# A two-layer trunk: eight row sums moved from the first gated network to attention's output product, two more inner tiles by block products, and the value weights at another offset

## The chip, the cores and the metric

The kernel runs on one core of a Trainium2 chip, in one launch. The metric is the device time of one execution in microseconds (us). The core has five engines that work side by side, each through its own list of instructions in order: PE multiplies matrices, DVE and ACT work on elements, POOL is a third and slower element engine, and SP only issues transfers. The program's order on each engine is fixed when it is built, so an instruction that waits holds up everything behind it on its engine.

## The reference, cut to what matters

```python
def adaln_params(c, w, b):
    mod = jax.nn.silu(c) @ w + b
    shift, scale, gate = jnp.split(mod, 3, axis=-1)
    ...
def modulate(x, g, shift, scale):
    return rmsnorm(x, g) * (1.0 + scale) + shift

def conv_ffn(h, w_up, conv_w, conv_b, w_down):
    up = h @ w_up
    a, b = jnp.split(up, 2, axis=-1)
    ...                                   # causal depthwise conv of width 3 on a
    return (jax.nn.silu(a_conv) * b) @ w_down

def reference(x, c, ...):
    h = x
    for i in range(DEPTH):                # 2 layers: S5 mixer, then forgetting attention
        shift, scale, gate = adaln_params(c, ada_w[i, 0], ada_b[i, 0])
        hn = modulate(h, norm_g[i, 0], shift, scale)
        m = s5_mixer(hn, ...) if i % N_MIXERS == 0 else fox_mixer(hn, ...)
        h = h + gate * m
        shift, scale, gate = adaln_params(c, ada_w[i, 1], ada_b[i, 1])
        hn = modulate(h, norm_g[i, 1], shift, scale)
        h = h + gate * conv_ffn(hn, ...)
    return rmsnorm(h, final_g)
```

The sequence has 512 positions, the model 1024 channels, the gated network 2816 inner channels, all in float32. The attention projects queries, keys, values and forget gates, makes a causal softmax over 16 heads and ends with an output product by a 1024 x 1024 matrix.

## The kernel before, in words

**Stages.** One after the other: the S5 mixer, the first gated network (below: the first network), attention (values, then eight pairs of heads with the projection of queries and keys between them, then the output product), the second gated network, and the last norm. The residual stream `h` stays on the chip as 8 channel tiles of 128 x 512.

**Products.** A float32 product is made of three products in a shorter format, `hi*hi + hi*lo + lo*hi`. So each weight that arrives (`raw`, 128 x 1024, or `rawd`, a single buffer of its own, for the down projection inside the first network) is split: ACT writes the rounded part `w_hi` (line 277), DVE the rest `w_lo` (line 278), and PE needs both. Line 294 holds the plain matmuls, 512 columns each or 256 in halves.

**Inner tiles.** The inner channels are 22 tiles, f = 0 to 21, in groups of 4, 4, 5, 4 and 5. A plain tile takes 48 matmuls of 512 columns. The others are made by `quarters()`: seven block products in place of eight, with 84 matmuls of 256 columns (line 550), four sums of weights on DVE (`sums`, line 518), a third split weight, and copies of block results by ACT (`nm_h`, line 557) which DVE combines (line 518 again). The tuple `plain` says which tiles are plain. The down projection of one group (line 294 too, and line 362 for the residual on DVE) is woven into the next group's inner tiles.

**Row sums.** The modulation parameters of later sub-layers are made in the background: `ada_units` (lines 217 to 260) has for each 128 channels a load of 512 KB (line 233) and one long DVE instruction that multiplies 128 x 1024 numbers and sums each row (line 247), and after eight of them one small addition (line 254). A call of `tick(n)` lets n steps of this list be recorded. With `late=True` a load is issued from POOL's queue after the sum that frees its buffer, with as many loads ahead as there are rooms; with `late=False` from SP's, one fewer ahead. The first network's list holds 32 row sums, two per inner tile from f = 4 on. Attention has three lists with 7, 7 and 2 sums, the last of them in the output product, at the evacuations of its tiles 4 and 5.

**Order.** A scheduling layer turns the recorded work into each engine's order by its own costs and due times. Therefore a change in the recorded steps also moves instructions around it.

**Places of split weights.** `part_of` gives each split weight a room of 9 x 128 elements, and the weight begins a few elements in: at `ASIDE` = 22 (88 bytes) where 256 columns are multiplied, at `VALUES` in attention's values (line 1366), where the split weights are the moving operand, with 256 or 272 columns.

**Output product.** `fox()` at its end multiplies by `fox_w_out`: the first four output tiles together (`head=4`, one step per k, between which the last pair of heads is finished), then tiles 4 and 5, and tiles 6 and 7 in halves (`tail=2`). The squares of the new `h` feed the next norm (lines 391 to 430), whose result `a_hi`, `a_lo` opens the second network.

Of the kernel before, what the change touches and what calls it, by code (L numbers as in the profile page):

```python
# [17 lines left out]
P = 128  # L18
D = 1024
KT = D // P  # L20
S = 512
# [28 lines left out]
units = lambda *thirds: [(i, t, j) for i, t in thirds for j in range(D // P)]  # L50
# [10 lines left out]
    pool.tile([P, n // 4], F32, name="fill", bufs=1)  # L61


ROOM, ASIDE, VALUES = 9 * P, 22, P - 22


def part_of(pool, shape, name, tag, bufs, aside=0):
# [1226 lines left out]
class Kernel(S5):  # L1294
# [93 lines left out]
    def fox(self, i, x, nxt):  # L1388
        with self.tc.tile_pool(name="fox", bufs=1, reuse_waits="tile") as pool:
            self.bgpool = pool  # L1390
            self.fox_heads(pool, x)
            after, y = nxt
            residual = self.add_residual(i)

            def add(m, ps, cols):
                residual(m, ps, cols)
                if m in (4, 5):
                    self.tick(1)

            self.product(  # L1400
                self.io["fox_w_out"], range(KT), KT, lambda k: (self.o[k][:, 0], self.o[k][:, 1]),
                add, head=4, tail=2, after=after, halves=(slice(0, S),), step=self.unit,
            )
        return y

# [133 lines left out]
def build(tc, io, out, stop=None):  # L1539
    with ExitStack() as ctx:  # L1540
        k = Kernel(tc, io, ctx)
        x = k.s5(0, k.norm_mod(1))
        if stop == "s5":
            return k.dump(out)
        k.done()
        k.bg = [k.ada_units(units(*((2, t) for t in range(3)), (3, 2)))]
        x = k.ffn(1, 0, x, k.norm_mod(2), ticks=1, plain=(0, 1, 2, 3, 6, 11, 17))
        k.done()
        k.bg = [
            k.ada_units(units((3, 1))[:7], rooms=("s3", "phi", "plo"), late=False),  # L1550
            k.ada_units(units((3, 1))[7:] + units((3, 0))[:6], rooms=(1, 2), late=False),
            k.ada_units(units((3, 0))[6:], rooms=("s3", "nf"), late=False),
        ]
        if stop == "ffn0":
            return k.dump(out)
        x = k.fox(2, x, k.norm_mod(3))
        k.done()
        k.mods.close()
        if stop == "fox":
            return k.dump(out)  # L1560
        k.ffn(3, 1, x, k.norm_out(out), plain=(0, 1, 2, 3))
        k.finish_norm()
# [83 lines left out]
```

## Time and profile before

| what | us |
|---|---|
| median of 3 runs | 1212.53 (1211.41 to 1212.78) |
| profiled execution, its own time | 1215.46 |
| span of that execution | 1213.7 |
| PE busy in it | 1183.8 (98%) |
| DVE busy | 1004.6 (83%) |
| ACT busy | 610.0 (50%) |
| POOL busy | 85.8 (7%) |
| row sums of the first network, first to last | 321.3 to 564.7 |
| attention's values (PE) | 617.8 to 668.0 |
| attention's output product, to the first matmul of the second network | 817.4 to 863.0 |

The page divides the span in 40 slices of 30 us. PE reads 9 (90% or more) in all but the first and the last slice, and DVE 7 to 9 in most. A row of the timeline has the start and the duration of an instruction in us, the engine, the line, what it writes and reads, and in brackets the engine's idle time before it with what ended it. A row of the windows has the length of the stretch and, for each engine, the busy time in it and the number of instructions, then the granted PE clock as a share, the share of busy transfer engines and GB/s.

### The profile page before, as it was taken

To read this page: it belongs to the slowest core of one execution; us is meant where nothing else is said; L and a number is where in the kernel's file an instruction comes from. 1 tells how busy PE (TensorE), PEld (TensorE's weight loads), DVE (VectorE), ACT (ScalarE), POOL (GpSimd) and SP (SyncE) were. 2 spreads that over 40 slices of the span, in tenths; PEclk is the share of its full clock that TensorE was granted. 3 is DMA by queue.
4 is the path that set the end of the run, shared out by engine and by line. 5 is a ranking of instruction groups with operands and counts; after the bars stand their busy time and mean duration, and the time that the engine had idled before them with its cause. 6 is when DMAs were issued, how large, how long until landed. Compare 5 with 4: busy or idle time off the path is not lost.

```text
span 1213.7 us, 20336 instructions
## 1 busy us (share of the span) xinstructions
PE 1183.8 (98%) x7793; PEld 1015.9 (84%) x7793; DVE 1004.6 (83%) x1872; ACT 610.0 (50%) x1156; POOL 85.8 (7%) x145
## 2 busy tenths in 40 slices
PE   6999999999999999999999999999999999999997
PEld 2566678898988899789899888878989999999987
DVE  7799987689899988899788578876899887888865
ACT  3554565335545453445443565764466554555543
POOL 0000000100000000000000343520000000000000
PEclk9899999999999999999999999999999999999999
DMA  9588787531364544544435453432213332333331
GB/s 356 188 266 258 245 271 253 202 99 53 122 204 156 179 163 155 161 159 130 131 125 194 162 173 134 150 109 88 89 55 111 117 121 84 104 103 109 109 100 70
DMA packets 74513, 183.81 MB, mean 151 GB/s; under 512 B 23232, under 2 KB 25632, under 8 KB 73392
## 3 DMA queue, kind: packets, MB, share of 16 engines
q1 hardware_dynamic: 68367, 161.02, 40.5%
q0 software_dynamic: 5760, 20.97, 5.4%
q8 instruction: 61, 1.00, 0.3%
q10 hardware_dynamic: 288, 0.52, 0.1%
q14 instruction: 37, 0.30, 0.1%
HBM read 175.57 MB, written 6.92 MB: 150 GB/s over the span
## 4 chain that ended last, share of the span: by engine, by line
PE 62%; issue 26%; DVE 4%; DMA 4%; POOL 2%; ACT 1%; SPq 0%; POOLq 0%; DVEq 0%; ACTq 0%
PE mmp L294 25%; PE mmp L550 11%; PE aux L550 4%; PE mmp L1174 3%; PE mmp L1366 3%; PE mmp L1203 2%; PE aux L1505 1%; PE aux L1525 1%; POOL ada_raw L233 1%; PE aux L1065 1%; PE mmp L205 1%; DMA ada_raw<-in_ada_t 1%; PE aux L978 1%; PE aux L1057 1%; DVE w_lo L278 1%
## 5 line engine op out<-in xcount | busy, mean ns | idle before, releaser
L278 DVE TENSOR_TENSOR w_lo<-raw,w_hi 128x1024 fp32r<-128x1024 f32 (+4 forms) x173 | 183.2, 1064 | 37.6 <-ACT w_hi L277 37.1
L277 ACT ACTIVATE w_hi<-raw 128x1024 fp32r<-128x1024 f32 (+4 forms) x173 | 154.8, 905 | 102.0 <-PE mmp L294 44.5
L294 PE MATMUL mmp<-ghi,w_hi 128*128 128x512 f32 (+1 forms) x392 | 145.1, 370 | 0.0
L294 PE MATMUL mmp<-ghi,w_lo 128*128 128x512 f32 (+1 forms) x392 | 144.3, 368 | 0.7 <-DVE w_lo L278 0.5
L294 PE MATMUL mmp<-glo,w_hi 128*128 128x512 f32 (+1 forms) x392 | 144.6, 369 | 0.0
L294 PE MATMUL mmp<-a_hi,w_hi 128*128 128x512 f32 (+1 forms) x376 | 138.4, 371 | 1.5 <-ACT a_hi L433 1.5
L294 PE MATMUL mmp<-a_hi,w_lo 128*128 128x512 f32 (+1 forms) x376 | 136.1, 362 | 0.3 <-DVE w_lo L278 0.3
L294 PE MATMUL mmp<-a_lo,w_hi 128*128 128x512 f32 (+1 forms) x376 | 135.7, 362 | 0.0
L550 PE MATMUL mmp<-w_hi 128*128 128x256 f32 x396 | 109.9, 278 | 3.0 <-ACT nm_h L557 2.5
L550 PE MATMUL mmp<-w_hi,w_lo 128*128 128x256 f32 x396 | 109.7, 278 | 0.7 <-DVE w_lo L278 0.7
L550 PE MATMUL mmp<-w_lo,w_hi 128*128 128x256 f32 x396 | 109.5, 277 | 0.0
L557 ACT ACTIVATE nm_h<-mmp 128x256 f32<-128x256 f32 x99 | 37.2, 381 | 108.3 <-PE mmp L550 108.3
L278 DVE TENSOR_TENSOR w_lo<-sums,w_hi 128x1024 fp32r<-128x1024 f32 x74 | 90.1, 1220 | 0.0
L277 ACT ACTIVATE w_hi<-sums 128x1024 fp32r<-128x1024 f32 x74 | 77.0, 1054 | 25.3 <-DVE sums L518 23.4
L294 PEld LDWEIGHTS mmp<-ghi,w_lo 128*128 128x128 f32 x392 | 74.2, 189 | 13.9 <-DVE w_lo L278 1.4
L294 PEld LDWEIGHTS mmp<-ghi,w_hi 128*128 128x128 f32 x392 | 74.2, 189 | 11.9 <-ACT w_hi L277 0.6
L294 PEld LDWEIGHTS mmp<-glo,w_hi 128*128 128x128 f32 x392 | 74.2, 189 | 11.0
L294 PEld LDWEIGHTS mmp<-a_hi,w_hi 128*128 128x128 f32 x376 | 70.2, 188 | 13.2 <-ACT a_hi L433 1.9
L294 PEld LDWEIGHTS mmp<-a_hi,w_lo 128*128 128x128 f32 x376 | 70.6, 188 | 12.5 <-DVE w_lo L278 1.3
L294 PEld LDWEIGHTS mmp<-a_lo,w_hi 128*128 128x128 f32 x376 | 70.7, 188 | 9.7
L362 DVE SCALAR_TENSOR_TENSOR h<-mmp,par,h 128x512 f32<-128x512 f32 (+1 forms) x100 | 68.1, 683 | 11.8 <-PE mmp L294 11.6
L550 PEld LDWEIGHTS mmp<-w_hi 128*128 128x128 f32 x396 | 74.5, 188 | 3.6 <-ACT nm_h L557 2.9
(319 smaller groups left out, 3082.2 us busy)
## 6 DMA issues: line engine op xcount, KB each, us to landing
raw<-in_w_up SPq DMA_DIRECT2D x88, 512.0 KB, 3.4
raw<-in_ada_w SPq DMA_DIRECT2D x40, 512.0 KB, 6.4
ada_raw<-in_ada_t POOLq DMA_DIRECT2D x40, 512.0 KB, 3.9
nf<-nfd SPq DMA_DIRECT2D x8, 1152.0 KB, 7.8
raw<-in_fox_qk SPq DMA_DIRECT2D x16, 512.0 KB, 3.6
raw<-in_w_down SPq DMA_DIRECT2D x24, 320.0 KB, 3.2
rawd<-in_w_down SPq DMA_DIRECT2D x24, 256.0 KB, 3.3
raw<-in_w_down SPq DMA_DIRECT2D x16, 384.0 KB, 3.4
```

The source lines that it names most:

```text
L205: self.last_mm = nc.tensor.matmul(ps[32 * qq:32 * qq + 32, :], self.sc32[:, k, :], w[:, q * S:(q + 1) * S], start=(step is steps[0]), stop ...
L233: (nc.gpsimd if late else nc.sync).dma_start(ws[n], src)
L277: nc.scalar.activation(hi, src, AF.Copy)
L278: return nc.vector.tensor_tensor(lo, src, hi.bitcast(F32), ALU.subtract)
L294: self.last_mm = self.nc.tensor.matmul(o, wt, xt[:, cols], start=(k == 0 and n == 0), stop=(k == nk - 1 and n == 2),)
L362: add = self.nc.vector.scalar_tensor_tensor(self.h[:, m, cols], ps, self.par[i][:, 16 + m:17 + m], self.h[:, m, cols], op0=ALU.mult, op1=A ...
L550: self.last_mm = nc.tensor.matmul(o, wt[:, k], xt[:, k], start=(first and k == 0 and n == 0), stop=(k == H - 1 and n == 2), skip_group_che ...
L557: a = nc.scalar.activation(t, o, AF.Copy)
L978: nc.tensor.matmul(ps[:, :, cols], x[:, q, r].rearrange("p c j -> p (c j)"), both[:, :, planes, q, :], start=(r == 0), stop=(r == 1), skip ...
L1174: nc.tensor.matmul(ps, w[m][:, k, :], x[:, k], start=(k == 0), stop=(k == KT - 1))
L1203: nc.tensor.matmul(gps[m], wt, xt[:, k], start=(k == 0 and part == 0 and xt is yhi), stop=(k == KT - 1 and part == 1))
L1366: self.last_mm = nc.tensor.matmul(ps[q, b][:, :n], xt[:, k, tb], wt, start=(k == 0 and i == 0), stop=(k == KT - 1 and i == 2),)
```

## The change

Three edits, which meet in the plan of the two stages.

1. Tiles f = 11 and f = 17 leave `plain`, so they too are made by block products.
2. The eight sums of unit (3, 2), the gate of the second network, leave the first network's list, which then has 24, and join attention's last list, which then has 10 in place of 2. This list is now `late=True`: its loads come from POOL's queue. Its steps are recorded at the seventh and eighth step of the first four output tiles (2 and 3 ticks) and at the evacuations of tiles 0 to 5.
3. `VALUES` goes from 106 elements (424 bytes) to 16 (64 bytes).

```diff
-ROOM, ASIDE, VALUES = 9 * P, 22, P - 22
+ROOM, ASIDE, VALUES = 9 * P, 22, 16
...
+            calls = []
+
+            def step(n=1):
+                self.unit(n)
+                calls.append(n)
+                if len(calls) in (KT - 1, KT):
+                    self.tick(2 + len(calls) - KT + 1)
+
             def add(m, ps, cols):
                 residual(m, ps, cols)
-                if m in (4, 5):
+                if m < 6:
                     self.tick(1)
...
-                add, head=4, tail=2, after=after, halves=(slice(0, S),), step=self.unit,
+                add, head=4, tail=2, after=after, halves=(slice(0, S),), step=step,
...
-        k.bg = [k.ada_units(units(*((2, t) for t in range(3)), (3, 2)))]
-        x = k.ffn(1, 0, x, k.norm_mod(2), ticks=1, plain=(0, 1, 2, 3, 6, 11, 17))
+        k.bg = [k.ada_units(units(*((2, t) for t in range(3))))]
+        x = k.ffn(1, 0, x, k.norm_mod(2), ticks=1, plain=(0, 1, 2, 3, 6))
...
-            k.ada_units(units((3, 0))[6:], rooms=("s3", "nf"), late=False),
+            k.ada_units(units((3, 0))[6:] + units((3, 2)), rooms=("s3", "nf")),
```

**How it moves instructions.** In the rows below stand the line, the operation, what is written from what, and the shape. `ISA` on line 247 is a row sum. Line numbers behind the edit are 8 higher in the changed kernel.

DVE in the output product, before, from the end of the last pair of heads (`ot` is its result, `v` the split of it; buffer numbers are kept, and the three `w_lo` are the weights of output tiles 5, 6 and 7):

```order
L1532 TENSOR_TENSOR ot_8709<-ot_8709,aux_8710 64x512
L1532 TENSOR_TENSOR ot_8709<-ot_8709,aux_8721 64x512
L278 TENSOR_TENSOR v_6346<-ot_8709,v_6346 128x512
...
L356 TENSOR_TENSOR ssq_8759<-ssq_8759,nm_t_8762 128x512
L278 TENSOR_TENSOR w_lo_8812<-raw_8813,w_hi_8811 128x1024
L356 TENSOR_TENSOR ssq_8759<-ssq_8759,nm_t_8766 128x512
L278 TENSOR_TENSOR w_lo_8849<-raw_8850,w_hi_8848 128x1024
L356 TENSOR_TENSOR ssq_8759<-ssq_8759,nm_t_8770 128x512
L278 TENSOR_TENSOR w_lo_8855<-raw_8856,w_hi_8854 128x1024
...
L247 ISA s3_8695,ada_s_7410<-s3_8695,c_row_1933 128x1024
```

and in the changed kernel (the instruction that stores each sum, and a few others, left out):

```order
L247 ISA nf_8803,ada_s_7516<-nf_8803,c_row_1933 128x1024
...
L247 ISA s3_8801,ada_s_7516<-s3_8801,c_row_1933 128x1024
...
L1540 TENSOR_TENSOR ot_8817<-ot_8817,aux_8818 64x512
...
L247 ISA nf_8858,ada_s_8873<-nf_8858,c_row_1933 128x1024
...
L278 TENSOR_TENSOR v_6452<-ot_8817,v_6452 128x512
L247 ISA s3_8855,ada_s_8873<-s3_8855,c_row_1933 128x1024
...
L247 ISA nf_8878,ada_s_8873<-nf_8878,c_row_1933 128x1024
...
L247 ISA s3_8875,ada_s_8873<-s3_8875,c_row_1933 128x1024
...
L278 TENSOR_TENSOR w_lo_8946<-raw_8947,w_hi_8945 128x1024
L247 ISA nf_8887,ada_s_8873<-nf_8887,c_row_1933 128x1024
...
L247 ISA s3_8881,ada_s_8873<-s3_8881,c_row_1933 128x1024
...
L278 TENSOR_TENSOR w_lo_8981<-raw_8982,w_hi_8980 128x1024
```

All ten row sums now stand between the last `plo` and the third `w_lo`: six ahead of the first `w_lo`, two between the first and the second, two between the second and the third. Of the two sums that stood here before, both came behind the third `w_lo`.

POOL at the end of the last pair of heads, before (line 1496 scales the softmax's rows) and in the changed kernel:

```order
L1453 TENSOR_TENSOR nf<-nf,rest 128x2x2x128
L1453 TENSOR_TENSOR nf<-nf,rest 128x2x256
L1496 TENSOR_SCALAR s_8581<-s_8581,sm 128x128 x2
L1496 TENSOR_SCALAR s_8591<-s_8591,sm 128x256 x2
L1496 TENSOR_SCALAR s_8601<-s_8601,sm 128x384 x2
L1496 TENSOR_SCALAR s_8611<-s_8611,sm 128x512 x2
```

```order
L1504 TENSOR_SCALAR s_8687<-s_8687,sm 128x128 x2
L1504 TENSOR_SCALAR s_8697<-s_8697,sm 128x256 x2
L233 DMA nf<-in_ada_t 128x1024
L1504 TENSOR_SCALAR s_8707<-s_8707,sm 128x384 x2
L1504 TENSOR_SCALAR s_8717<-s_8717,sm 128x512 x2
L233 DMA s_8801<-in_ada_t 128x1024
L233 DMA nf<-in_ada_t 128x1024
L233 DMA s_8855<-in_ada_t 128x1024
```

Ten loads of 512 KB are now issued from POOL, alternating between the rooms `nf` and `s`; before, two were issued from SP here.

ACT in the last group of inner tiles of the first network, around the block tile f = 18, before:

```order
L277 ACTIVATE w_hi<-rawd 128x512
L277 ACTIVATE ghi<-conv 128x512
L277 ACTIVATE w_hi<-rawd 128x512
L557 ACTIVATE nm_h<-mmp 128x256 x3
L277 ACTIVATE w_hi<-raw 128x1024
```

and in the changed kernel:

```order
L605 ACTIVATE conv<-conv 128x512
L277 ACTIVATE ghi<-conv 128x512
L557 ACTIVATE nm_h<-mmp 128x256 x3
L277 ACTIVATE w_hi<-rawd 128x512
L277 ACTIVATE w_hi<-raw 128x1024
```

The copies of block results (`nm_h`) stood behind the second split of the pair of `rawd` weights; now they stand ahead of it.

## The prediction, on record before the changed kernel ran

> **What bounds the kernel now.** I read the page's busy shares first, then windows stage by stage, then the rows around each stop of PE.
>
> ```profile
> span 1213.7 us, 20336 instructions
> PE 1183.8 (98%) x7793; PEld 1015.9 (84%) x7793; DVE 1004.6 (83%) x1872; ACT 610.0 (50%) x1156; POOL 85.8 (7%) x145
> ```
>
> PE sets the end: it is idle for 1213.7 - 1183.8 = 29.9 us in all. So a saving has to shorten PE's work or remove one of its few stops, and DVE, second at 83%, can make a new stop wherever it is filled. That is read by stage. The windows of the first network's groups 2 to 5 and of attention's values (PE, PEld, DVE, ACT, POOL busy, then clock, transfer share, GB/s):
>
> ```profile
> 305.29:366.60 61.31, 61.31 (x396) 55.63 (x395) 54.98 (x85) 30.42 (x49) 3.17 (x6) 1.00 0.52 165
> 366.60:439.63 73.03, 72.24 (x481) 65.44 (x480) 68.53 (x110) 35.57 (x58) 5.28 (x10) 1.00 0.53 174
> 439.63:507.87 68.24, 66.52 (x458) 60.74 (x457) 56.18 (x89) 30.69 (x51) 4.24 (x8) 1.00 0.44 145
> 507.87:579.21 71.34, 68.00 (x457) 62.33 (x456) 64.67 (x100) 32.50 (x54) 3.69 (x7) 0.98 0.47 151
> 617.76:668.00 50.24, 50.24 (x407) 49.50 (x407) 43.00 (x122) 21.57 (x40) 1.14 (x3) 1.00 0.50 168
> ```
>
> The group at 305 has no stop of PE with DVE at 90%. The one at 366 (f = 8 to 12, with the plain tile 11) has DVE at 68.53 of 73.03, 94%. The one at 507 (f = 17 to 21) has stops of 3.34 us and is the only one with a lower clock.
>
> **Term 1: what a tile gains.** Windows with the matmuls of one tile alone (PE, PEld, clock, transfers), a block tile, a plain tile, and the block tile f = 18:
>
> ```profile
> 320.18:329.73 9.55, 9.55 (x84) 9.50 (x83) 1.00 0.51 173
> 335.19:346.07 10.88, 10.88 (x49) 9.01 (x48) 1.00 0.73 239
> 522.09:536.04 13.95, 11.44 (x84) 11.21 (x83) 0.88 0.45 150
> ```
>
> A block tile takes 9.55 us and a plain one 10.88 (one of its 49 is a neighbour's): 1.33 us less PE work per tile, 2.7 for both, if DVE can follow. What it costs DVE, by the start-to-start times where DVE is full:
>
> ```profile
> 426.12 1.22 DVE L247 CUSTOM_DVE_ANT_0 ada_raw<-ada_raw,c_row 128x1024 f32<-128x1024 f32 x1
> 427.26 0.69 DVE L518 TENSOR_TENSOR sums<-sums,raw 128x512 f32<-128x512 f32 x1
> 427.86 0.69 DVE L518 TENSOR_TENSOR sums<-raw 128x512 f32<-128x512 f32 x1
> 432.80 0.42 DVE L518 TENSOR_TENSOR nm_t<-mmp,nm_h 128x256 f32<-128x256 f32 x1
> 433.13 1.22 DVE L278 TENSOR_TENSOR w_lo<-sums,w_hi 128x1024 fp32r<-128x1024 f32 x1
> ```
>
> From 426.12 to 427.26 is 1.14 for 1024 columns, to 427.86 is 0.60 for 512, 432.80 to 433.13 is 0.33 for 256. A block tile adds four sums (2.40) and four combinations (1.32), and splits 3.5 weights (1.14 + 1.14 + 1.14 + 0.60 = 4.02) where a plain tile splits two (2.28): 5.46 us in all. For the group at 366 this makes 68.53 + 5.5 = 74.0 us of DVE against 72.24 - 1.33 = 70.9 of PE. DVE is then the longer; its work may slip into the next group, where it has 68.24 - 56.18 = 12 us free. So f = 11 gives between -1.4 (all slips) and +2.5 (DVE's 74.0 plus the 1.5 it now leaves idle, against 73.03). I take -0.3, near the hidden end, because the group at 305 hides 90% wholly and this one must hide more.
>
> **Term 2: the last group.** Its largest stop:
>
> ```profile
> 523.59 0.69 DVE L278 TENSOR_TENSOR w_lo<-rawd,w_hi 128x512 fp32r<-128x512 f32 x1
> 524.30 5.31 SPq L183 DMA_DIRECT2D rawd<-in_w_down  x2
> 527.90 0.63 ACT L277 ACTIVATE w_hi<-rawd 128x512 fp32r<-128x512 f32 x1 [3.57 <-DMA rawd<-in_w_down]
> 528.44 0.64 ACT L557 ACTIVATE nm_h<-mmp 128x256 f32<-128x256 f32 x2
> 528.86 0.38 PE L550 MATMUL mmp<-w_hi 128*128 128x256 f32 x1 [2.50 <-ACT nm_h L557]
> 508.77 0.50 PE L294 MATMUL mmp<-a_hi,w_lo 128*128 128x512 f32 x1 [0.29 <-DVE w_lo L278]
> ```
>
> Read from the bottom of the chain: PE waits 2.50 for the copy `nm_h`. That copy stands on ACT behind a split that waits 3.57 for `rawd`, whose load could start at 524.30 only, once a late DVE had split the buffer's last content (523.59). The tile takes 13.95 instead of 9.55: 2.5 of stop and 1.9 at a granted clock of 0.88, 4.4 together. In the changed kernel DVE has eight row sums less here (8 x (1.14 + 0.08 of read-out) = 9.8) and 5.5 more for f = 17, so 64.67 - 4.3 = 60.4 against PE's 65.4 - 1.3 = 64.1 (65.4: 4 x 9.55 + 10.88 + 72 more matmuls of 10.88 / 48); and the copies stand ahead of that split. So I expect DVE in time: the group loses 71.34 - 65.4 = 5.9 now, of which the 4.4 and some 0.2 of the small stops go (4.6), and the tile's 1.33: -5.9. Its ends: -2.0, the tile's 1.33 and the small stops, if a like stop forms at another tile, as the group at 439 has 1.7 with DVE at 82%; -7.3 if every stop goes.
>
> **Term 3: the output product.** The rows of its DVE, and the one load that matters:
>
> ```profile
> 828.17 0.33 SPq L233 DMA_DIRECT2D s<-in_ada_t  x1
> 828.38 1.29 DVE L278 TENSOR_TENSOR plo<-aux,phi 128x512 fp32r<-128x512 f32 x2 [2.59 <-ACT phi L277]
> 832.77 0.68 DVE L1532 TENSOR_TENSOR ot<-ot,aux 64x512 f32<-64x512 f32 x1 [3.10 <-ACT ot L1531]
> 835.46 0.69 DVE L278 TENSOR_TENSOR v<-ot,v 128x512 fp32r<-128x512 f32 x1 [0.70 <-ACT v L277]
> 836.97 2.83 DVE L362 SCALAR_TENSOR_TENSOR h<-mmp,par,h 128x512 f32<-128x512 f32 x4 [0.82 <-PE mmp L294]
> 843.91 1.22 DVE L278 TENSOR_TENSOR w_lo<-raw,w_hi 128x1024 fp32r<-128x1024 f32 x1
> 860.27 0.87 DVE L430 SCALAR_TENSOR_TENSOR nm_h<-h,ga,aux 128x256 f32<-128x256 f32 x2 [0.47 <-PE aux L410]
> 862.96 0.36 PE L294 MATMUL mmp<-a_hi,w_hi 128*128 128x256 f32 x1
> ```
>
> DVE is free here: 2.59 + 3.10 + 0.70 + 0.82 us before 837, which is where eight more sums could go. But their loads come through two rooms, each refilled after its sum, and the row sums of the first network show that cycle:
>
> ```profile
> 522.99 0.08 DVE L247 DVE_READ_ACCUMULATOR2_ANT ada_s<- 128x1 f32 x1
> 523.37 0.53 POOL L233 DMA_DIRECT2D ada_raw<-in_ada_t  x1 [8.43 <-DVE ada_s L247]
> 527.22 1.22 DVE L247 CUSTOM_DVE_ANT_0 ada_raw<-ada_raw,c_row 128x1024 f32<-128x1024 f32 x1 [0.47 <-DMA ada_raw<-in_ada_t]
> ada_raw<-in_ada_t POOLq DMA_DIRECT2D x40, 512.0 KB, 3.9
> raw<-in_w_up SPq DMA_DIRECT2D x88, 512.0 KB, 3.4
> DMA to landing us min/median/max: 3.4/3.9/8.1
> ```
>
> A sum that has stored its result at 523.07 finds the next content at 527.22: 4.15, plus 1.22 + 0.08 for itself is 5.4 us per room. The `s` room is free at 828.17, as before; its first content is there at 828.17 + 3.9 = 832.1 and its five sums start at 832.1, 837.5, 842.9, 848.3 and 853.7. `w_lo` of tile 5 stands behind the third, with 0.60 and 0.66 between: done at 846.6. That of tile 6 is done at 852.0, and that of tile 7, behind the fifth, at 857.0; before it was 845.1 (843.91 + 1.22). A tile takes PE 24 x 10.88 / 48 = 5.4 us, the same as the cycle, so it stays just ahead of its weights; I put its three waits at 0.8, 0.5 and 0.5. Behind them on DVE come the splits for the second network (five, 5.7 us), the residuals and the eleven small steps of the norm, which before were done at 860.27. I put the first matmul of the second network at 869.4 instead of 862.96: +6.4, of which 1.8 is at the tiles and the rest waits for the norm. The ends: +2.1, if the loads are never late (10.0 us of sums less the 7.2 of holes just named, less 0.7 of idle later), and +9, if that wait also lowers the clock by what the 2.5 stop above did (1.9) and the splits all fall in front of the norm.
>
> The issues move from SP to POOL, behind scalings whose last row in the trace is this:
>
> ```profile
> 820.35 1.36 POOL L1496 TENSOR_SCALAR s<-s,sm 128x512 f32<-128x512 f32 x2
> ```
>
> They are done by 821.7; SP's queue gets shorter by two. Both cost nothing, because the rooms come free later than that; without this cover the first two sums would be 0.5 late, one issue.
>
> **Term 4: 64 bytes.** The rows of the values, and of another product, whose two operands begin at multiples of 64 bytes by the program's layout:
>
> ```profile
> 641.71 0.28 PE L1366 MATMUL mmp<-w_hi,a_hi 128*128 128x256 f32 x1
> 642.91 0.28 PE L1366 MATMUL mmp<-w_lo,a_hi 128*128 128x256 f32 x1
> 695.45 0.28 PE L1525 MATMUL aux<-phi,v 128*128 128x256 f32 x1
> 695.57 0.28 PE L1525 MATMUL aux<-plo,v 128*128 128x256 f32 x1
> ```
>
> The first two are ten steps apart: 120 ns each at 424 bytes. Line 1525 takes 120 ns too, while line 550 takes 9.55 / 84 = 114 with its stationary operand at 88 bytes. The nearest row, also with 256 columns as the moving operand, says that nothing changes: 0. The ends: +0.3, and -2.6, if 288 steps fall by 6.6 ns and the 96 wider ones by 7. [...]
>
> **The sum.** -0.3 - 5.9 + 6.4 + 0 = +0.2 on the profiled execution's 1215.46. That one lies 2.9 above the median 1212.53, so the forecast is 1212.7: no change that can be measured. For this kernel 0.2%, 2.4 us, is about what a measurement can tell from none.
>
> **Rivals.**
>
> *A, the loads are in time: faster.* The output product costs +2.1 only; then 1212.5 - 6.2 + 2.1 = 1208.4. For it: DVE's holes of 7.2 us, and a landing of 3.4 at the least, which makes the cycle 4.9. Against: with it the fifth sum of the `s` room still starts at 853.7 - 4 x 0.5 = 851.7, later than tile 7's weights were done. Chance 0.26.
>
> *B, the 64 bytes count.* -2.6 more: 1210.1. For it: line 550 shows that 256 columns can go in 114 ns. Against: line 1525. Chance 0.08.
>
> *C, the loads are late: slower.* The place is the `s` room's chain of four refills, and each is followed by `w_lo` on the same engine. A landing of 4.9 instead of 3.9 puts tile 7's weights and the norm 4 us later: 1216.7; the largest landing, 8.1, would add 4.2 for one refill. From 4.5 on it decides (4 x 0.6 = 2.4). For it: that maximum, and DVE full in front of each issue. Against: transfers are less busy here than in the groups above. Chance 0.21. [...]
>
> *D, the last group keeps its stop.* The single `rawd` buffer stays, and DVE's order may make it late at another tile: term 2 is then -2.0, and 1212.5 - 0.3 - 2.0 + 6.4 = 1216.6. For it: the group at 439 stops with DVE at 82%. Chance 0.07.
>
> **Numbers.** The forecast itself has 0.38, with a range of its own of 1209 to 1216. Of that 0.26 lies within 0.2%, 0.07 below and 0.05 above. A gives 0.25 faster, B 0.07, C and D together 0.27 slower, and each of these three 0.01 within. Together: faster 0.39, same 0.29, slower 0.32. The range of 1206 to 1219 holds A and C and most of the bounds: all four terms at one end together (1212.5 - 1.4 - 7.3 + 2.1 - 2.6 = 1203) are unlikely, and so is a load of 8 us in each cycle.
>
> **What will show it.** Term 1: line 550 at f = 11 in 9.6 us, DVE over 95% in that group, its length 73 or less. Term 2: no PE stop over 1 us after 508, and a length of 65 to 66. Term 3: row sums of one room 5.4 apart with a DMA as releaser, tile 7's `w_lo` near 857 less what was saved before, and a PE stop of 4 to 5 us ahead of the second network. Term 4: steps of line 1366 at 120. I am wrong if the output product adds less than 3 us or more than 9, or if the last group saves less than 3.

## The result, and the profile after

The changed kernel takes 1219.33 us (median of 18 runs, 1212.55 to 1227.79), the kernel before, on the same chips, 1212.18 (18 runs, 1209.63 to 1214.94). The ratio is 1.0057, with a 95% interval of 1.0042 to 1.0072: some 7 us slower. The forecast was 1212.7 with a range up to 1219. The profiled execution of the change was the fastest of its 18, so its page alone would have said the opposite:

```profile
span 1210.7 us, 20528 instructions
PE 1176.8 (97%) x7865; PEld 1014.9 (84%) x7865; DVE 1014.4 (84%) x1892; ACT 616.5 (51%) x1168; POOL 88.3 (7%) x147
```

PE is busy for 7 us less than before (1183.8), and the span is only 3 us shorter. Not all of the 7 is less work: the two tiles are worth 2.7 by term 1, and a matmul at a low clock counts as busy for longer (in the change, matmuls of 256 columns are 0.214 us apart and 0.41 long from 858.14 to 861.13, where the clock is at 0.50, and 0.115 apart and 0.28 long from 861.49 on, where it is at 1.00); the first profile of before has more low clock (last section). Because executions of one program differ, the stages below are means over three profiles each: of before, the one shown, one more, and that of a version with the same instruction order (the value weights at 64 bytes); of the change, the one shown and two more. The bounds are matmuls: the first block product, the first of line 1366, the last logits of the last pair of heads, the first matmul of the second network, the last matmul of all.

| stage | before, three profiles | change, three profiles | difference of the means |
|---|---|---|---|
| S5 and the first tiles | 299.9, 295.2, 295.6 | 294.3, 299.0, 299.2 | +0.6 |
| first network | 317.8, 317.4, 319.6 | 308.1, 308.4, 310.7 | -9.2 |
| values and heads | 199.3, 199.3, 199.1 | 198.5, 200.0, 198.9 | -0.1 |
| output product | 45.9, 45.8, 45.8 | 55.5, 56.1, 56.5 | +10.2 |
| second network and end | 342.8, 342.8, 343.8 | 346.5, 347.2, 346.2 | +3.5 |

The sum is +5.0, just below what the runs say (+5.1 to +8.7). The gain in the first network is larger than I forecast; the output product takes all of it, and the second network, whose own plan the change does not touch, loses 3.5 more.

The windows of the change for the groups from f = 4, 8, 13 and 17, and for the end of the first network, columns as in the prediction:

```profile
299.64:361.54 61.90, 61.53 (x396) 55.65 (x395) 55.23 (x85) 30.64 (x49) 3.18 (x6) 1.00 0.52 165
361.54:433.29 71.75, 68.87 (x508) 64.18 (x506) 69.03 (x114) 34.83 (x60) 5.30 (x10) 1.00 0.47 156
433.29:501.55 68.26, 68.26 (x467) 62.53 (x466) 65.31 (x102) 35.38 (x57) 3.72 (x7) 1.00 0.52 168
501.55:565.68 64.13, 64.13 (x493) 61.23 (x492) 56.60 (x88) 33.99 (x58) 0.00 (x0) 1.00 0.34 103
565.68:602.36 36.68, 35.25 (x222) 31.37 (x221) 26.30 (x53) 15.65 (x27) 0.00 (x0) 1.00 0.43 135
```

The last group went from 71.34 to 64.13 us without a single stop: DVE has 56.6 us of work in it instead of 64.67. In the group of f = 8 to 12 DVE is at 96%, and PE has two stops of about 1 us that were not there before, both for a late `w_lo`:

```profile
409.74 0.39 PE L550 MATMUL mmp<-a_hi,w_lo 128*128 128x256 f32 x1 [1.05 <-DVE w_lo L278]
419.05 0.50 PE L294 MATMUL mmp<-ghi,w_lo 128*128 128x512 f32 x1 [1.06 <-DVE w_lo L278]
```

Even so this group is 1.3 us shorter (71.75 against 73.03), because part of DVE's work slipped into the next one, where it is busy for 65.31 us instead of 56.18 and stops nobody.

Now the output product of the change. First DVE: the five sums of the `s` room, with all its waits for them grouped, then the split for output tile 7:

```profile
816.49 1.22 DVE L247 CUSTOM_DVE_ANT_0 s<-s,c_row 128x1024 f32<-128x1024 f32 x1 [1.69 <-DMA s<-in_ada_t]
821.84 1.23 DVE L247 CUSTOM_DVE_ANT_0 s<-s,c_row 128x1024 f32<-128x1024 f32 x1 [0.84 <-DMA s<-in_ada_t]
827.84 1.23 DVE L247 CUSTOM_DVE_ANT_0 s<-s,c_row 128x1024 f32<-128x1024 f32 x1 [0.93 <-DMA s<-in_ada_t]
833.24 1.23 DVE L247 CUSTOM_DVE_ANT_0 s<-s,c_row 128x1024 f32<-128x1024 f32 x1 [0.62 <-DMA s<-in_ada_t]
839.60 1.23 DVE L247 CUSTOM_DVE_ANT_0 s<-s,c_row 128x1024 f32<-128x1024 f32 x1 [0.42 <-DMA s<-in_ada_t]
841.49 1.22 DVE L278 TENSOR_TENSOR w_lo<-raw,w_hi 128x1024 fp32r<-128x1024 f32 x1
L247 DVE CUSTOM_DVE_ANT_0 s<-s,c_row 128x1024 f32<-128x1024 f32 x5 | 6.1, 1225 | 4.5 <-DMA s<-in_ada_t 4.5
```

The sums are 5.35, 6.0, 5.4 and 6.4 us apart, each behind a load. Behind them the norm of the second network has to pass DVE, step by step between splits of weights that it does not need yet (the first and the last step of the norm's root, and two splits between them):

```profile
848.51 0.15 DVE L391 TENSOR_SCALAR rs_v<-aux 128x2 f32<-128x2 f32 x1
849.82 1.22 DVE L278 TENSOR_TENSOR w_lo<-raw,w_hi 128x1024 fp32r<-128x1024 f32 x1 [0.16 <-ACT w_hi L277]
852.10 1.23 DVE L278 TENSOR_TENSOR w_lo<-raw,w_hi 128x1024 fp32r<-128x1024 f32 x1 [0.53 <-ACT w_hi L277]
853.83 0.16 DVE L401 TENSOR_TENSOR rs_y<-rs_y,rs_t 128x2 f32<-128x2 f32 x1
```

PE waits for that last step, and then runs slowly. The row of the waiting matmul before; then, in the change, its row and the window behind it, with the granted clock in the third column from the right:

```profile
859.55 0.68 PE L410 MATMUL aux<-rest,rs_y 128*128 128x128 f32 x4 [0.26 <-DVE rs_y L401]
```

```profile
854.13 0.81 PE L410 MATMUL aux<-rest,rs_y 128*128 128x128 f32 x4 [3.95 <-DVE rs_y L401]
854.13:864.13 10.00, 9.74 (x56) 9.45 (x57) 7.12 (x27) 4.07 (x8) 0.00 (x0) 0.66 0.16 57
```

The same window in the two other profiles of the change:

```profile
860.92:870.92 10.00, 9.73 (x46) 9.45 (x47) 6.85 (x26) 4.06 (x8) 0.00 (x0) 0.53 0.18 55
```

```profile
862.82:872.82 10.00, 9.74 (x51) 9.45 (x52) 6.85 (x26) 4.07 (x8) 0.00 (x0) 0.59 0.18 56
```

and the ten microseconds from the start of the second network before:

```profile
862.96:873.00 10.04, 9.58 (x82) 9.24 (x81) 8.48 (x27) 3.92 (x9) 0.00 (x0) 1.00 0.24 77
```

Before, matmuls of the last half tile stood behind the norm's matmul and filled the time until the norm was through (859.99 to 862.6); in the change they end at 850.2, ahead of it, and nothing is left to run. PE looks busy in both kernels, but in the change at 0.53 to 0.66 of the clock: 10 x (1 - 0.66) = 3.4, 4.7 and 4.1 us of work are lost behind a stop of about 4 us, some 1 us of it before the second network begins. This is the largest single item that the prediction had only at the end of its range. Most of the rest of the second network's loss is a stop between 1077 and 1087, in all three profiles of the change (1.20, 1.16 and 1.00 us) and in none of before:

```profile
1077.58 0.39 PE L550 MATMUL mmp<-w_hi 128*128 128x256 f32 x1 [1.20 <-ACT nm_h L557]
```

That stop does not come from the moved sums' place: the version with the sums among the heads (below) has it too, 1.21 us at 1076. What makes it was not tried.

### The profile page after: what moved, and what is told of

The parts are those of the page before. It is cut to its first block, busy times and chain, and to the rows that moved or that the text cites. A ratio compares the mean times of both kernels' runs of the same rounds, so it can differ in the third digit from the quotient of the medians.

```text
span 1210.7 us, 20528 instructions
## 1 busy us (share of the span) xinstructions
PE 1176.8 (97%) x7865; PEld 1014.9 (84%) x7865; DVE 1014.4 (84%) x1892; ACT 616.5 (51%) x1168; POOL 88.3 (7%) x147
## 4 chain that ended last, share of the span: by engine, by line
PE 58%; issue 19%; DVE 11%; DMA 8%; ACT 3%; POOL 1%; SPq 0%; DVEq 0%; POOLq 0%; ACTq 0%
PE mmp L294 23%; PE mmp L550 11%; PE aux L550 4%; DVE w_lo L278 3%; PE mmp L1174 3%; PE mmp L1366 2%; DMA raw<-in_w_up 2%; PE mmp L1203 2%; PE aux L1513 1%; PE aux L1065 1%; PE mmp L205 1%; PE aux L1057 1%; PE aux L978 1%; PE aux L1533 1%; DVE h L362 1%
## 5 line engine op out<-in xcount | busy, mean ns | idle before, releaser
L294 PE MATMUL mmp<-a_hi,w_hi 128*128 128x512 f32 (+1 forms) x344 | 127.0, 372 | 0.8 <-ACT a_hi L433 0.8
L294 PE MATMUL mmp<-a_lo,w_hi 128*128 128x512 f32 (+1 forms) x344 | 124.7, 363 | 0.3 <-DVE a_lo L434 0.3
L294 PE MATMUL mmp<-a_hi,w_lo 128*128 128x512 f32 (+1 forms) x344 | 124.4, 362 | 0.0
L550 PE MATMUL mmp<-w_hi 128*128 128x256 f32 x420 | 116.4, 277 | 2.4 <-ACT nm_h L557 1.8
L550 PE MATMUL mmp<-w_lo,w_hi 128*128 128x256 f32 x420 | 116.0, 276 | 0.0
L550 PE MATMUL mmp<-w_hi,w_lo 128*128 128x256 f32 x420 | 115.7, 276 | 0.0
L550 PEld LDWEIGHTS mmp<-w_lo,w_hi 128*128 128x128 f32 x420 | 78.9, 188 | 0.0
L550 PEld LDWEIGHTS mmp<-w_hi,w_lo 128*128 128x128 f32 x420 | 78.7, 188 | 0.0
L550 PE MATMUL mmp<-a_hi,w_lo 128*128 128x256 f32 x280 | 77.6, 277 | 1.1 <-DVE w_lo L278 1.1
L550 PE MATMUL mmp<-a_hi,w_hi 128*128 128x256 f32 x280 | 77.9, 278 | 0.4 <-ACT nm_h L557 0.4
```

Of the source, the lines that this page charges most:

```text
L294: self.last_mm = self.nc.tensor.matmul(o, wt, xt[:, cols], start=(k == 0 and n == 0), stop=(k == nk - 1 and n == 2),)
L550: self.last_mm = nc.tensor.matmul(o, wt[:, k], xt[:, k], start=(first and k == 0 and n == 0), stop=(k == H - 1 and n == 2), skip_group_che ...
```

## The experiments

**Each edit alone.** Three versions, each the kernel before with one of the edits.

```diff
# tiles alone
-        x = k.ffn(1, 0, x, k.norm_mod(2), ticks=1, plain=(0, 1, 2, 3, 6, 11, 17))
+        x = k.ffn(1, 0, x, k.norm_mod(2), ticks=1, plain=(0, 1, 2, 3, 6))
# values alone
-ROOM, ASIDE, VALUES = 9 * P, 22, P - 22
+ROOM, ASIDE, VALUES = 9 * P, 22, 16
# move alone: the lists of row sums and their ticks as in the change; plain and VALUES as before
```

> The kernel before with f = 11 and f = 17 as block tiles, and nothing else. Theory 1 (the eight row sums in the output product, and the low clock behind the stop they cause, are what made the change slower): with the row sums still in the first network, DVE has 64.7 + 5.5 = 70.2 us of work in the last group against 64.1 of PE, so the tiles' 2.7 us are mostly not gained; -2 to +2 us against before. Theory 2 (the two tiles themselves overfill DVE and stop PE in the first network, clock included): slower by 4 us or more, with run times that spread as those of the change do.

> The kernel before with the value weights at 64 bytes instead of 424, and nothing else; the instructions and their order stay. Theory 1: no difference, within 1 us of before, line 1366 still near 120 ns a step. Rival (the 64 bytes shorten the step towards 114 ns): 2 to 2.6 us faster. Theory 3 (the new place costs something of its own): slower.

> The kernel before with the eight row sums moved to the output product, f = 11 and 17 still plain, the value weights still at 424 bytes. Theory 1: the first network loses some 4 to 5 us of stops, the output product gains 11 us and more (the span of the profiled run of the change had 10.96 there), with a low granted clock behind its stop and a wide spread of run times: 5 to 13 us slower than before. Theory 2 (the move is harmless, the tiles are not): as fast as before or faster.

Measured: tiles 1215.39 (ratio 1.0021, 1.0000 to 1.0043), values 1213.65 (0.9991, 0.9976 to 1.0007), move 1217.80 (1.0038, 1.0020 to 1.0056). So +2.5, -1.1 and +4.6 us, together +6.0 where the change has +6.9. The values' new place does nothing that can be told from none; the step of line 1366 keeps its rate, 166 weight loads in 20 us with either place (windows of line 1366 alone, before and then the new place):

```profile
638.00:658.00 20.00, 20.00 (x167) 19.84 (x166) 1.00 0.67 228
```

```profile
635.00:655.00 20.00, 19.89 (x167) 19.69 (x166) 1.00 0.64 226
```

The moved sums alone lose 4.6, a little less than the 5 to 13 that theory 1 gave. In that version's profile the stop ahead of the second network is 3.14 us and the ten microseconds from that network's start at 866.34 have a clock of 0.69; its output product takes 53.8, its second network 344.2. The tiles alone do not gain, as theory 1 said, and may lose a little more than it allowed. But their profile (the fastest of the 12 runs) has a first network of 314.9, 3.4 us shorter than before, which the median does not confirm; where its slower executions lose, up to 1223.46, was not profiled. Alone, tiles and move shorten the first network by 3.4 and 1.7 us in their profiles, together by 9.2. This points to two edits that need each other, but it is one profile each, and some 3 us of the difference is a low clock at the end of the first network in the move's profile (0.92 from 570.34 to 611.90).

**A second profile of the change.** The same kernel once more.

> The changed kernel once more, for a second profile: its profiled run was the fastest of 18, with a mean clock of 0.995, where most had 0.992 and below. Theory 1: an execution near the median of 1219 shows the same busy times as the fast one, a stop of PE of about 4 us ahead of the second network, and more time at a low granted clock behind it; the first network as in the first profile. Theory 2: the added time lies at stops in the first network, in the groups of f = 8 to 12 or 17 to 21.

Its time was 1220.54, and theory 1 held: first network 308.4 again, output product 56.1, a stop of 4.04 us and a clock of 0.53 behind it, as quoted above.

**The stop filled.** Matmuls without use, put behind the last half tile of the output product, where PE would stand still:

```diff
                     evac(m, ps, c)
+                    if step and c is HALVES[1] and m == last[-1]:
+                        idle = self.mm.tile([P, S], F32, name="mmp")
+                        for n in range(22):          # 2 in the control
+                            self.nc.tensor.matmul(
+                                idle[:, :S // 2], wk[m][n % nk][0], x(n % nk)[0][:, c], start=True, stop=True,
+                            )
```

> The change, with 22 matmuls of 256 columns into a buffer that nobody reads, put on PE behind the last half tile of the output product and ahead of the wait for the norm: 2.5 us of work in a stop that took 4.1 us in both profiles of the change. Theory 1 (a part of the cost is the granted clock, 0.66 in the 8 us behind that stop): the clock stays at 1.00 there, the second network starts at the same time but runs 2 to 3 us shorter at its start; 2 to 3 us faster than the change. Rival (only the wait itself costs): as the change, within 1 us, or slower by the 2.5 us of the added work.

> The version with the filled stop, with 2 matmuls in place of 22: the same recorded steps, so nearly the same order behind them, but the stop ahead of the second network stays open by some 4 us. Theory (the filled stop won its 6.7 us against the change mostly by the clock): low clock behind the stop again, and 4 us or more slower than the filled version. Rival (the added steps changed the order of the second network, where the stops at 1076 and 1094 went away, and this is what won): within 1.5 us of the filled version.

Measured: 1212.62 with 22 (ratio to before 1.0001, 0.9987 to 1.0016), 1219.46 with 2 (1.0053, 1.0033 to 1.0072). Twenty useless matmuls make the kernel 6.3 us faster by the two ratios, more than twice what theory 1 gave. In the profile of the control, the wait and the window behind it:

```profile
861.10 1.20 PE L416 MATMUL aux<-rest,rs_y 128*128 128x128 f32 x4 [3.82 <-DVE rs_y L407]
861.10:871.10 10.00, 9.74 (x57) 9.45 (x58) 7.22 (x27) 4.08 (x8) 0.00 (x0) 0.67 0.17 57
```

and with the filled stop:

```profile
857.98 2.66 PE L339 MATMUL mmp<-v,w_hi 128*128 128x256 f32 x22
860.47 0.60 PE L416 MATMUL aux<-rest,rs_y 128*128 128x128 f32 x4
860.47:870.47 10.00, 9.52 (x82) 9.21 (x81) 9.05 (x32) 6.24 (x12) 0.00 (x0) 1.00 0.16 47
```

The clock stays at 1.00, which is 3.3 us in these ten alone. Not all of the 6.3 is the clock: with 22 matmuls the scheduler also put one split of weights behind the norm's steps instead of between them, so PE waits for nothing at 860.47, and three stops of the second network (0.63, 1.16 and 0.83 us at 902, 1085 and 1103 in the control) are not there. In these two profiles the clock is about half and these the rest; how they divide exactly is left open.

**The loads taken away.** The ten sums use their first two contents again, so this kernel leaves out the gate of the second network and a part of one more parameter; DVE has the same ten sums:

```diff
         def load(n):
+            if reuse and len(rooms) <= n < len(todo):
+                ws[n] = kept[n % len(rooms)]
+                return
             if n < len(todo):
```

> The change, where the ten sums of attention's last list use the first contents of their two rooms again and again in place of eight more loads, so the gate of the second network and part of one more parameter are not computed; DVE has the same ten sums. Theory 1 (the cycle of sum and reload in two rooms sets DVE's pace): without waits for loads, 5.0 us in the first profile of the change, the output product takes 48 to 51 us instead of 55.5, the stop ahead of the second network shrinks to under 1 us and its low clock goes; 5 to 8 us faster than the change. Rival (DVE's own ten sums and the splits behind them are the bound): less than 2 us faster.

Measured: 1213.93 (1.0017, 1.0001 to 1.0033), 5 us faster than the change. The wait ahead of the second network is gone, as theory 1 said, but the output product still takes 54.5 us, not 48 to 51: the sums now stand in one block ahead of a residual and of the split for the next tile, and PE stops there, at once with a low clock:

```profile
837.75 0.50 PE L298 MATMUL mmp<-v,w_hi 128*128 128x256 f32 x2 [1.83 <-DVE h L366]
840.71 0.80 PE L298 MATMUL mmp<-v,w_lo 128*128 128x512 f32 x1 [2.45 <-DVE w_lo L282]
835.00:850.00 15.00, 10.67 (x48) 8.65 (x46) 11.02 (x16) 4.40 (x6) 0.00 (x0) 0.77 0.42 140
```

So both were half right. Without the reload cycle the long stop does not form, and ten sums in this order delay PE without it too.

**f = 11 plain again** in the change (`plain=(0, 1, 2, 3, 6, 11)`).

> The change with f = 11 plain again. Both profiles of the change show stops of 1.2 and 1.2 us at 408 and 417 in the group of f = 8 to 12, which the kernel before does not have. Theory 1 (DVE is the bound in that group, so the tile's 1.3 us are given back): as the change, within 1.5 us. Theory 2 (the tile costs more than it gives, by late loads and low clocks): 2 us and more faster than the change. If the tile's gain is real, 1.3 us slower than the change.

Measured: 1218.54 (1.0051, 1.0031 to 1.0071, 6 runs), the change's own time within 1 us. The tile neither gains nor costs what can be told from six runs. That its 1.3 us of PE work go into the two stops shown above, as theory 1 had it, is not shown: in this version's only profile the first network takes 312.8 us, 3.7 more than the change's mean, and the output product 55.0, 1.0 less.

**The eight sums among the heads.** The change, with the eight sums at the end of attention's second list, the third list and the output product as before:

```diff
-                self.tick(1)                       # in turn(), behind the last block
+                self.tick(2)
...
-            k.ada_units(units((3, 1))[7:] + units((3, 0))[:6], rooms=(1, 2), late=False),
+            k.ada_units(units((3, 1))[7:] + units((3, 0))[:6] + units((3, 2)), rooms=(1, 2), late=False),
```

> The change with the eight row sums in another place: they join attention's second list, two sums per pair of heads in place of one, loaded through SP into spare weight buffers; the output product is as in the kernel before. DVE is busy for about 15 us of the 19 of a pair in the kernel before, so 1.2 more fits. Theory 1 (the first network's 10 us, seen in both profiles of the change, are real and only the output product eats them): first network 308, heads 137 to 139, output product 46: 6 to 9 us faster than before. Theory 2 (the block tiles f = 11 and 17 lose in most executions what they gain in the profiled ones): within 2 us of before.

Measured: 1210.85 (0.9995, 0.9979 to 1.0011), by the ratios 7.5 us faster than the change, and no faster than before. The first network (310.6) and the output product (45.9) did what theory 1 said; the heads did not: 203.7 us from the first value to the last logits, 4.4 more than before. In five pairs PE waits for `ot` from DVE, as in the first row, with 0.72 us from start to start where the neighbours have about 0.2. The two sums, on DVE, take almost twice their 1.22 us, as in the next two rows; the last row is POOL adding its mask at that time:

```profile
727.88 0.44 PE L1483 MATMUL aux<-hi 64*128 64x384 f32 x1 [0.28 <-DVE ot L1540]
739.77 2.17 DVE L247 CUSTOM_DVE_ANT_0 raw<-raw,c_row 128x1024 f32<-128x1024 f32 x1
741.87 2.31 DVE L247 CUSTOM_DVE_ANT_0 raw<-raw,c_row 128x1024 f32<-128x1024 f32 x1
739.56 3.53 POOL L1461 TENSOR_TENSOR nf<-nf,rest 128x512 f32<-128x512 f32 x2 [3.77 <-DMA nf<-nfd]
```

**The second sum of a pair earlier.** The same, with one tick behind the second block and one behind the last:

```diff
-            if b == NB - 1:
+            if b in (1, NB - 1):
                 self.evac = [part.ins]
-                self.tick(2)
+                self.tick(1)
```

> As the version with the eight sums among the heads, but the second sum of a pair is recorded after the second block's transposes instead of right behind the first sum. In that version's profile a sum took 2.1 to 2.3 us wherever POOL added its mask at the same time (POOL 3.53 instead of 2.55), and 1.2 us elsewhere; the heads took 141.3 us instead of 137.2. Theory (the two engines slow each other, and the stops of 0.62 us per pair come from that): the moved sum takes 1.2 us, the heads take 138 to 139, and the whole is 2 to 3 us faster than that version, 3 to 5 us faster than before. Rival (any second sum delays a pair by so much): as that version.

Measured: 1204.47 us (1200.70 to 1208.62, 6 runs), ratio to before 0.9929, 0.9901 to 0.9956: 8.6 us faster than before, more than I expected, and 15 us faster than the change. Values and heads take 196.7, the first network 309.0, the output product 45.8. Both sums of a pair are back at about 1.22 us (1.40 at most), the waits for `ot` are gone, and what collides with POOL is one split:

```profile
717.05 1.22 DVE L247 CUSTOM_DVE_ANT_0 raw<-raw,c_row 128x1024 f32<-128x1024 f32 x1
718.19 2.31 DVE L278 TENSOR_TENSOR w_lo<-raw,w_hi 128x1024 fp32r<-128x1024 f32 x1
715.73 3.69 POOL L1461 TENSOR_TENSOR nf<-nf,rest 128x512 f32<-128x512 f32 x2 [3.41 <-DMA nf<-nfd]
```

**Two more profiles**, one of before and a third of the change.

> The kernel before, for another profile. Theory: what differs between executions of one program is the granted clock behind stops of 1 to 3 us (the start, 526, the end of the first network near 605): some executions show a stretch below 0.9 there and some do not, 1.5 to 5 us each; the lengths of the stages agree within 1 us once that is taken off. Rival: lengths differ at a full clock too.

> The change, for a third profile. Theory: the stop ahead of the second network is 4 us and the clock behind it is low as in the two others; the first network, 308 us in both, is 310 to 313 in some executions, by a low clock behind its stops at 408 to 420 or at its end, as in the other kernels that share its first network. Rival: it is 308 again and the added time lies elsewhere.

Their times were 1210.12 and 1221.32. The stages of before agree within 0.5 us with the first profile's except for the start, 295.2 against 299.9. By the clock records of the traces the first has 17.1 us at half the clock ahead of its end and the second 6.8; half of the difference is 5.1 us, and the spans differ by 5.3. The third profile of the change has the clock down from 20 to 60 us (0.87), in the last 41 us of the first network (0.96) and behind the stop (0.59), but not at 408 to 420, which had been named too; its first network takes 310.7.

## Why the prediction was wrong

**What bounds the kernel.** Right: PE sets the end, and DVE decides where PE stops. What changed came through DVE's order and, behind the stops, through the clock.

**Terms 1 and 2, the first network.** The direction was right and the size too small: -6.2 forecast, -9.2 measured. The last group lost 7.2 us where I took 5.9; every stop went, which was the low end of that term. The group of f = 8 to 12 gained 1.3 where I took 0.3, with DVE's surplus slipping into the next group as the hidden end assumed. (The other end, +2.5, counted 1.5 us of idle DVE where the row has 73.03 - 68.53 = 4.5; it should have been +5.5.) Two microseconds more came at the end of the network (38.55 us from the last group's end to the values before, 36.68 after), where before's clock was 0.96 in both profiles and the change's 1.00 in this one and 0.96 in the third. Most of that part is the clock's chance and no merit of the term.

**Term 3, the output product.** Here the prediction failed. +6.4 was forecast for the whole way to the second network's start and nothing behind it; it measures +10.2, more than the 9 that I had named as a sign of being wrong, and +3.5 behind it. The mechanism was the one named: two rooms, each refilled after its sum, `w_lo` and the norm behind the sums in DVE's order. The cycle of 5.4 us measured 5.35 to 6.4, so tile 7's split ended at 842.71, which is 41.9 us after the last logits where I had 857.0 - 817.1 = 39.9. The first matmul of the second network came another 1.2 us later, of which 0.9 is already the low clock (0.60 over the 2.17 us from the norm's matmul on). What was mis-sized most is the clock: I held a low clock for the far end of this term, at 1.9 us, from a stop of 2.5 us that I had in front of me, and put it at nothing in the sum. A stop of about 4 us brought 3.4, 4.7 and 4.1, in each profile. With their mean, 4.1, in the sum the whole would have been about +4.3. Of the 7.3 us that +6.4 lacks to +10.2 and +3.5, the clock is thus about 4.1, the late refills 2.0 in the first profile, and the stop between 1077 and 1087 about 1.1.

**Term 4.** Right: the 64 bytes change nothing, 0.9991. The row of line 1525, which also starts at multiples of 64 bytes and took 120 ns, told it.

**The rivals.** A (loads in time) fell: DVE waited 4.5 us for the `s` room alone, and even the version without reloads is 2.1 us slower than before, not 4 faster. B fell with the unchanged step of line 1366; its -2.6 lies just within the interval of the times. D fell: the last group kept no stop. C (late loads) had the right place and came near the time with 1216.7, in part by luck: two of the four refills were late, by 0.6 and 1.0 us, where C had all four late by 1, and the rest of its 4 us was the clock. Without any reload 5 of the 7 us go, and the sums alone still stop PE. What none of them held is that the stop ahead of the second network is paid for twice, with 4.0 to 4.4 us of waiting and with 3.4 to 4.7 us at a low clock.

## What to carry to other kernels

A stop of the matmul engine cost more than its own length here: behind each of the six stops of 3.1 to 4.4 us came ten microseconds at a clock of 0.53 to 0.69, which is another 3.1 to 4.7 us lost. A forecast for this kernel should add it, and work without use in the stop was cheaper than the stop: with 22 such matmuls the kernel took 1212.62 us, with 2 of them 1219.46. An engine's idle time in a stage is not room for more work when what stands behind that work in its order is what the next stage waits for: the same eight sums cost 14 us in the output product and behind it, 4.4 in one place among the heads, and nothing that can be seen with one sum of each pair a few rows earlier. And one profile of a kernel whose executions differ by several microseconds says little on its own: here the slower kernel's first profile had the shorter span.

## What the runs showed of the hardware

**The clock behind a stop.** Stops of 3.1 to 4.4 us were followed by a clock of 0.53 to 0.69 over ten microseconds in each of the six profiles that have one ahead of the second network (three of the change, the moved sums alone, f = 11 plain, the control of the filled stop; the ten are counted from the norm's matmul; for the moved sums, 0.69, and for f = 11 plain, 0.68, they are counted from the second network's start). In the clock records of the first profiles of before and of the change each low stretch is at 0.50. Behind the stop of the change's first profile it lasts 6.83 us, from 854.55 to 861.38; by the windows it is about as long in three of the other five, and about 10 us in the second and third profile of the change.

Behind a shorter stop it came in some executions and not in others. At the block tile f = 18 the first profile of before had 0.88, and the second 1.00, with nearly the same stop, 2.50 and 2.43 us (windows of line 550 alone; the row of the first stands in the prediction, this is the second):

```profile
518.00:532.00 14.00, 10.04 (x84) 9.83 (x84) 1.00 0.46 153
```

Behind a stop of 1.64 us at 606.90 the first profile of before had 3.41 us at 0.50, from 608.42 on.

**The start.** The clock is low at times where nothing was changed, too. From 20 to 60 us, the first and the second profile of before, and the first of the change:

```profile
20.00:60.00 40.00, 37.54 (x158) 19.08 (x153) 32.89 (x90) 15.99 (x42) 0.00 (x0) 0.87 0.67 242
```

```profile
20.00:60.00 40.00, 38.87 (x169) 19.75 (x170) 36.10 (x84) 19.69 (x55) 0.00 (x0) 0.96 0.77 279
```

```profile
20.00:60.00 40.00, 37.55 (x177) 19.45 (x177) 37.70 (x92) 20.24 (x57) 0.00 (x0) 1.00 0.78 283
```

40 x 0.13 = 5 us, or 1.6, or none. The start is 4.7 of the 5.3 us between before's two profiled executions; what spreads the other runs was not profiled. The change has both lengths too (294.3, 299.0 and 299.2 us), so the -5.6 of its first profile against the first of before, at the start, belongs to neither kernel.

**DVE and POOL.** A row sum reads `raw` and `c_row`, which the program keeps in SBUF, and takes 1.22 us. It took up to 2.31 where one of POOL's additions to `nf`, which lies in SBUF too, had begun first: in the first profile of before 2.31 at 786.91, 0.07 us behind the start of an addition, and 1.76 at 693.49, 0.62 behind one. Where the sum began first it kept its 1.22 and POOL's addition took longer: in the first profile of the change the sum at 751.70 took 1.22, and the addition at 752.02 took 2.06, where one takes 1.29 with no row sum or split beside it. Instructions that read one of their operands from PSUM, such as `plo<-aux,phi`, kept their time beside POOL: 0.69 and 0.68 us at 785.70 and 786.31 in the first profile of before, during an addition of 1.29 that began at 785.58. What makes the two engines slow each other was not shown. The version that moved one sum per pair by a few rows, and so has one such collision in a pair instead of two, has values and heads 7.0 us shorter in its profile (196.7 against 203.7); that all of this comes from the collisions was not tried, nor why its values and heads, with eight sums more, are 2.5 us shorter than before's.
